# A hybrid encoder layer: the recurrence's inputs scaled in the stage before it, head sums token-major, two inverses in one run

## The chip, the cores and the metric

The kernel runs on one core of one Trainium2 chip. The metric is the device time of one launch in microseconds (us), lower is better. TensorE (PE), VectorE (DVE), ScalarE (ACT) and GpSimd (POOL) each work through their own queue in order. All transfers are issued by SyncE (SP), also in order.

## The reference

One layer of a bidirectional encoder is applied to two groups with shared weights: 1024 prompt tokens and 256 sample tokens, 1280 in all, model width 1024, fp32. What the change touches is the RWKV-7 branch of the token mixer: 8 heads of size 64, a forward and a backward scan with their own decay `w` and rate `a`.

```python
kk = heads(k32 * k_k)
kk = kk / jnp.maximum(jnp.linalg.norm(kk, axis=-1, keepdims=True), 1e-12)
for d, (z, z_shift, rev) in enumerate(...):
    ...
    w = jnp.exp(-jnp.exp(-jax.nn.softplus(-logit) - 0.5))
    a = jax.nn.sigmoid(iclr_a0[d] + za @ iclr_a2[d])
    kd = k32 * (1.0 + (a - 1.0) * k_a)
    outs.append(_wkv_scan(heads(r32), heads(w), kk, kk * heads(a), heads(kd), heads(v32), rev))
# one step of the scan, per head, S is 64 x 64
sa = S @ kk_t
S = S * w_t - sa b_t^T + v_t k_t^T
y_t = S @ r_t
...
bonus = jnp.sum(heads(r32) * heads(k32) * r_k, axis=-1, keepdims=True) * heads(v32)
```

Around it stand the input projection (1024 to 5888 columns), a gated convolution branch, two output projections, a gated ConvFFN and a gated embedding.

## The kernel before, in words

The scan is done in chunks of 64 tokens. Inside a chunk the decays are folded into the inputs: with P the running product of decays, the kernel needs q = r P, c = kk P(previous), k = kd / P and b = -kk a / P. A Gram product of (b, k) with (c, q) gives triangular 64 x 64 matrices. One of them must be inverted. POOL inverts its 32 x 32 diagonal blocks by elimination, 31 multiply-add pairs in a chain; two small PE products fill in the off-diagonal block.

**Stage one** projects and prepares. PE works through a list of blocks (`Fill`): one block is 128 output columns for all 1280 tokens, 72 matmuls into tile `mm`. Between its matmuls the code places other work. `go(us)` runs so much planned fill; `run_side()` empties a list of small closures (`side`) that otherwise go one at a time each `fill.pace` us of fill. For each of the four head pairs `hp` there is a k block and an r block. Then come `lora` products in psum tile `sm` for both directions d and two kinds (0: decay logit, 1: rate a), the sum of squares of kk over each head (`kk_norm`) and the bonus sum (`bonus`). Both sums are PE products of a [128 channels, 1280 tokens] operand, split into high and low halves (`halve`: tiles `gl`, `t`), with a block of ones (`bo`, `ind`). The closures write L (log decay, cumulated by a DVE scan), kd, nb, kk and r to DRAM (`to_in`, tensors d_in and d_kr). The big work tiles of this stage come from a ring `o5` of four, the others from a ring `t5` of three.

**The recurrence** has 20 steps n (10 groups of 128 tokens forward, 10 backward), two chunks in each. A step's own chain alternates small PE products with short copies on ACT and DVE:

- `b_x2`: AT with Dm, copied by ACT; `b_m21`: the result with MT, copied by ACT into MT.
- For each chunk: `c_p1` (tile p, copied to R), `c_sa` (R with MT, copied to SV), `c_z` (SV with ZL; DVE adds it to the state Sc and scales it into the next SV). After the second chunk SP stores the step's output (d_y from Y).
- For later steps: `a_prep` loads X (d_in, d_kr), takes two exponentials on ACT and makes K = (b, k) and LS = (c, q) by seven DVE products. `a_gram(n, h)` makes Gram half h: eight PE products, six masked DVE copies into AT, LS and ZL. `a_t` transposes K. SP sends AT to DRAM (dA) and back in another layout (`load_u`, tiles U and W). POOL runs `b_inv` (tiles tm and W). SP sends W out (dW, `b_out`) and back into MT (`b_back`), and DVE transposes it (`b_d`, tile Dm).

In step n the code places the Gram and the inverse for n+2, the way back of the inverse for n+1, and `a_prep` for n+3. `gap(us)` spreads the fill that is left evenly over the steps (gates and convolution blocks, 72 matmuls each). From step 11 on each step also has a group norm for one finished token group, on DVE and ACT (`gn`, tiles cvp, cvy, gr...), handed out by the second argument of `gap`. Nearly every engine instruction is issued through a wrapper that keeps program order; its one line is L199 before and L205 after, so groups are told apart by their tiles.

Of the kernel before, what the change touches and what calls it, by code (L numbers as in the profile page):

```python
# [12 lines left out]
D = 1024  # L13
# [112 lines left out]
def build(tc, I, O, dbg=None, upto=99):  # L126
# [10 lines left out]
    def to_in(d, nm, hp, t, w=128):  # L137
        dst, o = (d_in[d], 0) if nm in ("L", "kd", "nb") else (d_kr, 386)
        SP.dma_start(dst[hp * 128:(hp + 1) * 128, :, IN[nm][0] - o:IN[nm][1] - o], t.rearrange("p (g t) -> p g t", t=w))
# [27 lines left out]
    d_in = [dram([DC, NT, 386], f"d_in{d}") for d in range(2)]  # L167
    d_kr = dram([DC, NT, 256], "d_kr")
    IN = dict(L=(0, 130), kd=(130, 258), nb=(258, 386), kk=(386, 514), r=(514, 642))
# [38 lines left out]
    wq = pool("wq", 1, side="right")  # L208
    p1 = pool("p1", 1, side="right")
# [84 lines left out]
    class VBlock:  # L294
# [110 lines left out]
    zs, ks, kks, kns, S1 = {}, {}, {}, {}, {}  # L405
# [58 lines left out]
    def halve(nm, t):  # L464
        def hi():
            S1[nm] = sb(p1b, [128, T], F32R, "gl"), sb(p1, [128, T], F32R, "t5", 3)
            A.copy(S1[nm][0], S1[t])
        return [hi, lambda: V.tensor_tensor(S1[nm][1], S1[t], S1[nm][0].bitcast(F32), ALU.subtract)]

    def ones(ps, w, hl):  # L470

        for t0, n in TTS:
            for q in range(2):
                PE.matmul(ps[:, t0:t0 + n], w, hl[q][:, t0:t0 + n], start=q == 0, stop=q == 1)

    def k_block(hp):
# [6 lines left out]
        def done():  # L483
            kk = kks[hp] = sb(p1b, [128, T], F32, "kk", 1)

            def square():
                S1["kk2"] = sb(p1, [128, T], F32, "t5", 3)
                A.activation(S1["kk2"], kk, AF.Square)
            side([lambda: V.tensor_scalar(kk, ks[hp], pc("k_k", hp), None, ALU.mult), square,
                  lambda: to_in(0, "kk", hp, kk)])  # L490
        return Block(OFF["k"] + hp * 128, ev, begin, done)

    def kk_norm(hp):

        ps = sb(psm, [128, 3 * 512], F32, "sm")
        ones(ps, S1["bo"], S1["sq"])
        n2 = kns[hp] = sb(p1, [128, T], F32, "t5", 3)
        V.tensor_scalar(n2, ps[:, 0:T], 1e-24, None, ALU.max)
        side([lambda t=t: V.reciprocal(n2[:, t:t + 320], n2[:, t:t + 320]) for t in range(0, T, 320)])
        side([lambda: V.tensor_tensor(n2, n2, kks[hp], ALU.mult)])  # L500

    def r_block(hp):
        def begin():
            S1["r"] = sb(p1, [128, T], F32, "o5", 4)

        def ev(ps, t0, n, po):
            A.copy(S1["r"][:, t0:t0 + n], ps)

        def done():
            side([lambda: to_in(0, "r", hp, S1["r"])])  # L510
        return Block(OFF["r"] + hp * 128, ev, begin, done)

    def rk_prep(hp):
        def product():
            S1["rkk"] = sb(p1, [128, T], F32, "t5", 3)
            V.scalar_tensor_tensor(S1["rkk"], S1["r"], pc("r_k", hp), ks[hp], ALU.mult, ALU.mult)
        side([product])

    def bonus(hp):

        if hp == 0:
            S1["bn"] = sb(p1b, [128, T], F32, "bn")
        rows = slice(32 * hp, 32 * hp + 32)
        run_side()
        ps = sb(psm, [128, 3 * 512], F32, "sm")
        ones(ps[0:32], S1["ind"], S1["rk"])
        A.copy(S1["bn"][rows], ps[0:32, 0:T])

    def bonus_t(i, n):

        ps = sb(pt, [128, 4, 128], F32, "tp")
        for j in range(n):
            PE.transpose(ps[:, j, :], S1["bn"][:, (i + j) * 128:(i + j + 1) * 128], ident)
        V.tensor_copy(bon[:, i:i + n, :].rearrange("p i (q h) -> p i h q", q=2),
                      ps[:, 0:n, :].rearrange("p i (h x) -> p i h x", x=32)[:, :, :, 0:2])
# [14 lines left out]
    def lora(d, hp, which):  # L550
# [9 lines left out]
        if which == 0:  # L560
            L = sb(p1, [128, NCH, 65], F32, "o5", 4)
# [61 lines left out]
    items[-1].ahead = items[-1].every = 2  # L623
# [3 lines left out]
    for j in range(8):  # L627
# [335 lines left out]
    blocks = sb(wq, [128, 128], F32, "gth", 2)  # L963
    SP.dma_start(cs1, I["consts"][:, C_SCAN:C_BO])
    SP.dma_start(blocks, I["consts"][:, C_BO:C_WI])
    for nm, t in (("bo", blocks), ("ind", ind)):
        S1[nm] = sb(p1b, [128, t.shape[1]], F32R, nm)
        A.copy(S1[nm], t)

    def mix(n, jobs, lead=0.0, used=0.0):  # L970

        go(lead)
        run_side()
        for j in jobs:
            j()
            go((12.6 - lead - used) / len(jobs))
        fill.until(n + 1)

    def rates(hp):

        js = [lambda d=d, w=w: lora(d, hp, w) for d in range(2) for w in range(2)]
        js.insert(2, lambda: rk_prep(hp))
        js.insert(4, lambda: side(halve("rk", "rkk")))
        return js
# [5 lines left out]
    js = [lambda i=i: g_out(i) for i in range(NT)]  # L990
    for d in range(2):
        js.insert(3 + 4 * d, lambda d=d: lora_split(d))
    mix(2, js, 3.0)
    for hp in range(4):
        if hp > 0:
            mix(2 + 2 * hp, rates(hp - 1), 0.9)
        go(1.7)
        if hp > 0:
            bonus(hp - 1)
        side(halve("sq", "kk2"))  # L1000
        mix(3 + 2 * hp, [lambda: kk_norm(hp)], 6.0, 1.7)
# [17 lines left out]
    LS = [sb(wk, [128, 3, 8, 64], F32, f"LS{i}") for i in range(3)]  # L1019
# [1014 lines left out]
```

## Time and profile before

| what | value |
|---|---|
| median of three runs | 2251.77 us (2249.8 to 2258.03) |
| the profiled execution, its own time | 2248.55 us |
| its span, first to last instruction | 2246.8 us |
| mean granted TensorE clock | 0.982 |
| PE busy | 2143.3 us, 95% |
| DVE, ACT, POOL busy | 1455.8, 872.4, 613.0 us |
| first and last `b_x2` product of the recurrence | 354.9 and 920.0 us |

A time is read from the start of the span. In a table of stretches each engine's busy time stands beside its count of instructions, then the granted clock, the share of time the DMA engines were busy, and GB/s. The rows come with the prediction.

### The profile page before, as it was taken

Reading aid. Unit: us, or ns where it says so; the run is one execution under the profiler, and the core shown is the slowest. Engines: PE = TensorE matmul, PEld = TensorE weight load, DVE = VectorE, ACT = ScalarE, POOL = GpSimd, SP = SyncE. Lnnn points to the kernel's source line nnn. Section 1 sums busy time; section 2 is a strip of 40 time slices with the busy share of each in tenths; the row PEclk is TensorE's granted clock in tenths of the full one; section 3 lists DMA queues with packets and bytes.
Section 4 is the critical chain, followed back from the end, with each engine's and each line's share of the span. In section 5 each row is a group of like instructions: output and inputs, shape, how many; then the busy total and the mean of one; then the engine's idle time right before and its main releaser. Section 6 shows DMA issues by size and latency. Waiting matters only on the chain.

```text
span 2246.8 us, 40106 instructions
## 1 busy us (share of the span) xinstructions
PE 2143.3 (95%) x15895; PEld 1855.1 (83%) x15895; DVE 1455.8 (65%) x2325; ACT 872.4 (39%) x1531; POOL 613.0 (27%) x1370
## 2 busy tenths in 40 slices
PE   6999999999999889999997999999999999999998
PEld 5877887878777777888886999999999888887886
DVE  5488845655556775565576687777677755556565
ACT  4533222333344444431444444444444521113444
POOL 3024337888787777100000000000000011115000
PEclk9999999999999999999998999999999999999999
DMA  4456664445456665553445532122212442233121
GB/s 152 125 125 157 160 182 130 115 121 150 138 158 172 198 181 138 183 178 137 141 132 168 146 98 74 62 72 71 73 62 88 139 146 85 85 111 130 43 72 62
DMA packets 333975, 278.58 MB, mean 124 GB/s; under 512 B 93693, under 2 KB 297307, under 8 KB 333787
## 3 DMA queue, kind: packets, MB, share of 16 engines
q1 hardware_dynamic: 333787, 276.01, 41.0%
q8 instruction: 125, 2.05, 0.4%
q14 instruction: 63, 0.52, 0.1%
HBM read 192.50 MB, written 83.44 MB: 123 GB/s over the span
## 4 chain that ended last, share of the span: by engine, by line
PE 54%; DVE 8%; POOL 5%; DMA 4%; issue 3%; ACT 2%; SPq 2%; ACTq 0%; POOLq 0%; DVEq 0%
PE mm L199 22%; PE X L199 12%; PE Y L199 9%; PE g L199 6%; POOL W L199 3%; POOL tm L199 3%; SPq L199 2%; PE p L199 2%; DMA dA<-AT 1%; DVE h L199 1%; DVE wl L199 1%; DVE cvp L199 1%; PE m L199 1%; DVE aj L199 1%; PE tp L199 1%
## 5 line engine op out<-in xcount | busy, mean ns | idle before, releaser
L199 PE MATMUL mm<-U,wh 128*128 128x512 f32 (+1 forms) x1872 | 530.3, 371 | 2.8 <-ACT U L199 2.3
L199 PEld LDWEIGHTS mm<-U,wh 128*128 128x128 f32 x1872 | 326.4, 192 | 64.0 <-issue 3.7
L199 PE MATMUL mm<-U,wl 128*128 128x512 f32 (+1 forms) x936 | 338.4, 362 | 1.0 <-POOL wl L199 1.0
L199 POOL TENSOR_TENSOR MG<-raw,MG 128x1024 fp32r<-128x1024 f32 x5 | 12.1, 2417 | 974.5 <-ACT MG L199 974.5
L199 POOL TENSOR_TENSOR tm<-W,U 128x60 f32<-128x60 f32 (+24 forms) x620 | 225.6, 364 | 122.2 <-DMA W<-in_consts 63.6
L199 POOL TENSOR_TENSOR W<-W,tm 128x60 f32<-128x60 f32 (+24 forms) x620 | 234.6, 378 | 48.6
L199 DVE TENSOR_TENSOR f<-f,mm 128x512 f32<-128x512 f32 x200 | 136.3, 686 | 104.3 <-PE mm L199 103.1
L199 PEld LDWEIGHTS mm<-U,wl 128*128 128x128 f32 x936 | 179.0, 191 | 29.9 <-POOL wl L199 1.5
L199 PE MATMUL mm<-MG,act 128*128 128x512 f32 x600 | 159.9, 393 | 2.0 <-DVE f L199 1.9
L199 DVE SCALAR_TENSOR_TENSOR h<-MGb,fcol,h 128x255 f32<-128x255 f32 (+1 forms) x176 | 152.5, 880 | 14.3 <-ACT h L199 12.5
L199 PE MATMUL X<-B,wh 128*128 128x384 f32 (+1 forms) x936 | 158.4, 315 | 2.6 <-DVE MGb L199 2.6
L199 ACT CAST wh<-raw 128x512 fp32r<-128x512 f32 (+1 forms) x141 | 113.8, 808 | 118.1 <-PE Y L199 41.6
L199 PEld LDWEIGHTS X<-B,wh 128*128 128x128 f32 x936 | 144.2, 189 | 3.2 <-DVE MGb L199 3.2
L199 PE MATMUL X<-B,wl 128*128 128x384 f32 (+1 forms) x804 | 137.1, 315 | 2.9 <-DVE MGb L199 2.9
L199 PEld LDWEIGHTS mm<-MG,act 128*128 128x128 f32 x600 | 113.8, 190 | 26.4 <-DVE f L199 2.6
L199 PEld LDWEIGHTS X<-B,wl 128*128 128x128 f32 x804 | 123.7, 190 | 3.2 <-DVE MGb L199 3.1
L199 PE MATMUL mm<-wh,MG 128*128 128x512 f32 x400 | 126.2, 394 | 0.0
L199 PE MATMUL g<-WG,MG 128*128 128x512 f32 x480 | 112.8, 391 | 0.0
L199 PEld LDWEIGHTS g<-WG,MG 128*128 128x128 f32 x480 | 89.4, 188 | 18.3
L199 DVE TENSOR_TENSOR wl<-raw,wh 128x1024 fp32r<-128x1024 f32 (+1 forms) x68 | 79.7, 1172 | 23.6 <-ACT wh L199 23.3
L199 PEld LDWEIGHTS mm<-wh,MG 128*128 128x128 f32 x400 | 74.8, 187 | 18.4
L199 PE MATMUL Y<-B,wh 128*128 128x384 f32 x420 | 85.1, 335 | 0.0
(494 smaller groups left out, 4274.6 us busy)
## 6 DMA issues: line engine op xcount, KB each, us to landing
raw<-in_w_up SPq DMA_DIRECT2D x53, 512.0 KB
raw<-in_w_in SPq DMA_DIRECT2D x39, 512.0 KB
X<-d_in SPq DMA_DIRECT2D x20, 772.0 KB
d_act<-h SPq DMA_DIRECT2D x22, 640.0 KB
MGb<-d_act SPq DMA_DIRECT2D x20, 640.0 KB
raw<-in_w_down SPq DMA_DIRECT2D x22, 512.0 KB
d_in<-o SPq DMA_DIRECT2D x16, 640.0 KB
X<-d_kr SPq DMA_DIRECT2D x20, 512.0 KB
```

Of the source, the lines that this page charges most:

```text
L199: return lambda *a, **k: tc.keep_in_program_order(f(*a, **k))
```

## The change

Five things change together.

1. **Scaled inputs.** The two exponentials and the products with P and 1/P move from the recurrence (`a_prep`, removed) into stage one (`scaled_inputs`). Stage one stores k and b (d_bk, already in the layout of tile K, in runs of 64 floats) and c and q (d_cq). The recurrence loads K and LS by DMA alone (`load_k`, `load_l`). The end-of-chunk decays stay on chip in `pend`. The multiplications by k and by the normalized kk go from POOL to DVE, three affine steps from DVE to ACT.
2. **Head sums token-major.** `by_head` takes 128 channels x 128 tokens as the stationary operand and two columns of ones as the moving one, ten matmuls for 1280 tokens, in place of `ones` on split halves. The reciprocal then runs on 20 elements of each partition instead of 1280; `kk_norm` spreads it back over the channels by ACT copies and ten PE transposes. `bonus_t` and `halve` are gone.
3. **Two inverses in one run.** U, W and tm hold two steps. `b_inv(m)` does steps 2m and 2m+1 with the same 62 POOL instructions, each twice as large.
4. **Grams three to four steps ahead.** Odd steps make the Grams for n+3 (at the old place) and n+4 (late in the step), even steps none. POOL starts a run at the start of an even step; its result goes out in the odd step.
5. **Two gate blocks** of fill are moved from the recurrence to the time before it.

```diff
+    def by_head(x):
+        ps = sb(pt, [128, 512], F32, "tp")
+        for i in range(NT):
+            PE.matmul(ps[:, 2 * i:2 * i + 2], x[:, i * 128:(i + 1) * 128], ind[:, 0:2], start=True, stop=True)
...
+    def kk_sum(hp):
+        run_side()
+        r = S1["rn"] = sb(p1, [128, NT, 2], F32, "rn")
+        V.tensor_scalar(r, by_head(S1["kk2"]), 1e-24, None, ALU.max)
+        V.reciprocal(r, r)
     def kk_norm(hp):
         ps = sb(psm, [128, 3 * 512], F32, "sm")
-        ones(ps, S1["bo"], S1["sq"])
...
-        side([lambda t=t: V.reciprocal(n2[:, t:t + 320], n2[:, t:t + 320]) for t in range(0, T, 320)])
+        for i in range(0, NT, 4):
+            n = min(4, NT - i)
+            rb = sb(wq, [128, 4, 128], F32, "gth", 2)[:, 0:n]
+            A.copy(rb.rearrange(...), S1["rn"][:, i:i + n].unsqueeze(3).broadcast_to((128, n, 2, 64)))
+            for j in range(n):
+                PE.transpose(ps[:, (i + j) * 128:(i + j + 1) * 128], rb[:, j], ident)
+        V.scalar_tensor_tensor(kns[hp], ps[:, 0:T], -0.5, kks[hp], ALU.mult, ALU.mult)
...
+        def k_out():
+            V.tensor_tensor(S["kd"], S["kd"], S["Pi"], ALU.mult)
+            to_in(d, "k", hp, S["kd"])
...
+        return [affine, lambda: V.scalar_tensor_tensor(a, a, 1.0, kn, ALU.add, ALU.mult),
+                lambda: V.tensor_tensor(S["kd"], S["kd"], k, ALU.mult), inverse, decay, k_out, b_out, q_out, c_out]
...
-            mix(2 + 2 * hp, rates(hp - 1), 0.9)
...
+    rates = lambda d, hp: [(0.9, lambda: lora(d, hp, 0)), (1.5, lambda: lora(d, hp, 1))]
+            rk_prep(hp - 1)
+            mix(2 + 2 * hp, rates(0, hp - 1) + [(8.5, lambda: bonus(hp - 1))])
+        mix(3 + 2 * hp, (rates(1, hp - 1) if hp > 0 else [(2.4, run_side)])
+            + [(3.0, lambda: kk_sum(hp)), (5.0, lambda: kk_norm(hp))])
...
+            G.tensor_tensor(tm[:, :, cs, js], W[:, :, cs, i:i + 1].broadcast_to(shape), Ut[:, :, i:i + 1, js].broadcast_to(shape), ALU.mult)
+            G.tensor_tensor(W[:, :, cs, js], W[:, :, cs, js], tm[:, :, cs, js], ALU.add)
...
+        if not odd:
+            if n + 2 < N:
+                load_u(n // 2 + 1)
+                b_inv(n // 2 + 1)
+            b_back(n + 1)
...
+        if odd and n + 3 < N:
+            a_gram(n + 3, 0)
...
         c_z(n, 1)
+        load_l(n + 4)
+        if nx:
             load_v(n + 2)
-        gap(0.7, 1)
-        side(a_prep(n + 3))
-        gap(4.2)
+            if odd:
+                b_out(n // 2 + 1)
+                b_back(n + 1)
+        gap(4.9, 1)
+        if odd and n + 4 < N:
+            for h in range(2):
+                a_gram(n + 4, h)
+        gap(3.0)
         if nx:
             b_d(n + 1)
-        gap(6.7, 1)
+        gap(3.7, 1)
```

DVE in stage one, the second direction of one head pair, before (SCALAR_TENSOR_TENSOR with `cs` is the scan; `t_1273` is the norm of the next pair, `o_1134` L, `o_1171` a, `o_1172` kd):

```order
L199 TENSOR_SCALAR o_1134<-o_1134 128x20x64
L199 SCALAR_TENSOR_TENSOR o_1134<-cs_588,o_1134 128x1300
L199 TENSOR_TENSOR t_1153<-t_1125,gl 128x1280
L199 TENSOR_SCALAR o_1172<-o_1171,half 128x1280
L199 TENSOR_SCALAR o_1171<-o_1171 128x1280
L199 TENSOR_SCALAR kk<-k,pcol 128x1280
L199 TENSOR_TENSOR t_1234<-t_1216,gl 128x1280
L199 TENSOR_TENSOR wl<-raw,wh 128x1024
L199 TENSOR_SCALAR t_1273<-sm 128x1280
L199 RECIPROCAL t_1273<-t_1273 128x320 x4
L199 TENSOR_TENSOR t_1273<-t_1273,kk 128x1280
```

The same place after (`o_1220` is L and then q, `o_1241` a and then b, `o_1246` kd and then k, `cvy` 1/P and then c, `o_1269` P, `rn` the 20 norms):

```order
L205 SCALAR_TENSOR_TENSOR o_1220<-cs_590,o_1220 128x1300
L205 SCALAR_TENSOR_TENSOR o_1241<-o_1241,t_1038 128x1280
L205 TENSOR_TENSOR wl<-raw,wh 128x1024
L205 TENSOR_TENSOR o_1246<-o_1246,k 128x1280
L205 TENSOR_TENSOR o_1246<-o_1246,cvy 128x1280
L205 TENSOR_TENSOR o_1241<-o_1241,cvy 128x1280
L205 TENSOR_TENSOR o_1220<-cvp,o_1269 128x1280
L205 TENSOR_TENSOR cvy<-kk,o_1269 128x1280
L205 TENSOR_SCALAR rn<-tp 128x20
L205 RECIPROCAL rn<-rn 128x20
L205 SCALAR_TENSOR_TENSOR t_1339<-sm,kk 128x1280
```

The long reciprocal is gone, and the two small instructions on `rn` now stand behind the five products of the second direction.

ACT at the same place after (`kk` and `t_1208` are kk and its square for the next pair, `sm,half` the two tanh that empty `sm`):

```order
L205 ACTIVATE kk<-k,pcol 128x1280
L205 ACTIVATE t_1208<-kk 128x1280
L205 ACTIVATE o_1220<-sm,half 128x20x64
L205 ACTIVATE o_1220<-o_1220 128x20x64
L205 CAST wh<-raw 128x1024
L205 ACTIVATE o_1241<-sm,half 128x1280
L205 ACTIVATE o_1246<-o_1241,half 128x1280
```

Before, kk came from DVE; now kk and its square stand on ACT ahead of the tanh that frees `sm` for the second product.

SP in the second half of an odd step, after (LS is loaded in three pieces; dW and MT are the inverse's way out and back, dA the late Gram's way out):

```order
L205 DMA K<-d_bk_58 128x4x256
L205 DMA d_thr<-gth 128x256
L205 DMA d_y_64<-Y 64x2x256 x2
L205 DMA LS_2206<-d_cq_60 64x4x128 x2
L205 DMA LS_2206<-d_cq_60 128x4x128
L205 DMA SV<-d_v 64x2x256 x2
L205 DMA dW<-W 512x1x32 x4
L205 DMA MT_2207<-dW 32x8x32 x4
L205 DMA dA<-AT 32x8x32 x4
```

Before, dW and MT stood ahead of d_y in every step and the X loads behind SV; now the load that the late Gram needs stands behind the step's own store.

More of the change, by code (lines that the diff above doesn't have):

```diff
@@ L165, in build @@
     dram = lambda shape, tag: dr.tile(shape, F32, name=tag, tag=tag)
[L167 to L169 removed]
+    d_bk = [dram([DC, NT, 256], f"d_bk{d}") for d in range(2)]
+    d_cq = [dram([DC, NT, 256], f"d_cq{d}") for d in range(2)]
     d_v, d_g = dram([2, T, 256], "d_v"), dram([2, T, 256], "d_g")
@@ L208, in build @@
     wq = pool("wq", 1, side="right")
+    pend = sb(wq, [128, 2, 4, NCH], F32, "pend")
     p1 = pool("p1", 1, side="right")
@@ L462, in g_out @@
         SP.dma_start(d_g[:, tk, :].rearrange("q t m -> t q m"), gt.rearrange("t (q m) -> t q m", q=2))
[L464 to L474, printed above, removed]
+    def by_head(x):
+        ps = sb(pt, [128, 512], F32, "tp")
+        for i in range(NT):
+            PE.matmul(ps[:, 2 * i:2 * i + 2], x[:, i * 128:(i + 1) * 128], ind[:, 0:2], start=True, stop=True)
+        return ps[:, 0:2 * NT].rearrange("p (i q) -> p i q", q=2)
     def k_block(hp):
@@ L515, in product @@
             S1["rkk"] = sb(p1, [128, T], F32, "t5", 3)
-            V.scalar_tensor_tensor(S1["rkk"], S1["r"], pc("r_k", hp), ks[hp], ALU.mult, ALU.mult)
+            V.scalar_tensor_tensor(S1["rkk"], rs_[hp], pc("r_k", hp), ks[hp], ALU.mult, ALU.mult)
         side([product])
     def bonus(hp):
-        if hp == 0:
-            S1["bn"] = sb(p1b, [128, T], F32, "bn")
-        rows = slice(32 * hp, 32 * hp + 32)
         run_side()
[L525 to L535, printed above, removed]
+        V.tensor_copy(bon.rearrange("p i (q h) -> p i q h", q=2)[:, :, :, hp], by_head(S1["rkk"]))
     def lora_load(d):
@@ L622, in build @@
         items += [k_block(hp), r_block(hp)]
-    items[-1].ahead = items[-1].every = 2
+    items += [gate(0, 0), gate(1, 0)]
+    items[-1].ahead, items[-1].every = 20, 1
     items += [VBlock(0), VBlock(1)]
@@ L626, in build @@
         items += conv(i)
-    for j in range(8):
+    for j in range(1, 8):
         items += [gate(0, j), gate(1, j)]
@@ L962, in build, with mix @@
     cs1 = sb(p1b, [128, 1300], F32, "cs1")
-    blocks = sb(wq, [128, 128], F32, "gth", 2)
     SP.dma_start(cs1, I["consts"][:, C_SCAN:C_BO])
[L965 to L974, printed above, removed]
+    def mix(n, jobs):
+        for us, j in jobs:
+            go(us)
             j()
-            go((12.6 - lead - used) / len(jobs))
         fill.until(n + 1)
[L979 to L984, printed above, removed]
     fill.until(2)
@@ L1303, in group_norm @@
         SP.dma_start(d_ob[tk, :], y2)
-    load_x(0)
-    go(17.0)
-    side(a_prep(0))
-    run_side()
-    go(5.0)
-    for h in range(2):
-        a_gram(0, h)
-        go(1.2)
-    load_u(0)
-    b_inv(0)
-    a_t(0)
-    go(1.2)
-    side(a_prep(1))
-    go(11.0)
-    run_side()
-    for h in range(2):
-        a_gram(1, h)
-        go(1.2)
-    load_u(1)
-    a_t(1)
-    go(1.2)
-    go(8.0)
+    load_k(0)
+    for n in range(4):
+        load_l(n)
+    go(6.0)
+    for n in range(4):
+        for h in range(2):
+            a_gram(n, h)
+            go(1.2)
+        if n == 1:
+            load_u(0)
+            b_inv(0)
+        if n < 3:
+            a_t(n)
+            load_k(n + 1)
+            go(6.0)
+    go(5.0)
     b_out(0)
     b_back(0)
-    b_inv(1)
-    side(a_prep(2))
-    go(10.0)
-    b_d(0)
-    go(2.0)
-    fill.until(12)
+    fill.until(14)
     load_v(0)
@@ L1337, in build @@
     go(4.0)
+    b_d(0)
     gn = iter(())
```

228 lines of the change are left out of this document (109 added, 119 removed).

## The prediction

> **What bounds the kernel now.** I read the table of slices first (PE is busy 95% of the span), then stretches, since only two stages are touched: stage one (about 108 to 300 us) and the recurrence (355 to 950 us). Columns: length, busy time and count of PE, PEld, DVE, ACT and POOL, granted clock, DMA share, GB/s.
>
> ```profile
> core 0: us, PE busy (x) PEld busy (x) DVE busy (x) ACT busy (x) POOL busy (x), PEclk, DMA share, GB/s
> 150.00:193.00 43.00, 38.71 (x180) 30.04 (x179) 36.31 (x20) 14.46 (x16) 15.15 (x6) 0.96 0.59 145
> 193.00:236.00 43.00, 39.31 (x181) 30.41 (x181) 40.67 (x22) 15.97 (x18) 15.17 (x6) 0.96 0.64 148
> 236.00:300.00 64.00, 61.01 (x440) 56.37 (x441) 37.82 (x27) 16.15 (x21) 14.20 (x5) 0.95 0.68 177
> 355.00:671.00 316.00, 304.27 (x3914) 245.46 (x3912) 181.16 (x346) 111.98 (x251) 253.81 (x690) 0.98 0.51 135
> 671.00:950.00 279.00, 258.48 (x3139) 208.67 (x3139) 177.63 (x358) 127.75 (x255) 174.44 (x475) 0.95 0.61 174
> 413.00:440.00 27.00, 26.31 (x354) 21.37 (x353) 19.32 (x32) 9.30 (x21) 22.77 (x55) 1.00 0.39 109
> 585.00:590.00 5.00, 3.74 (x59) 3.52 (x60) 3.34 (x6) 1.10 (x3) 4.29 (x10) 0.81 0.52 122
> 590.00:595.00 5.00, 5.00 (x101) 4.08 (x100) 2.37 (x6) 2.26 (x6) 3.98 (x14) 0.85 0.91 295
> 1000.00:1050.00 50.00, 50.00 (x260) 42.75 (x259) 30.40 (x52) 10.18 (x19) 0.00 (x0) 1.00 0.35 120
> ```
>
> PE bounds nearly all of it, so only PE's idle time and lost clock can be won, or PE work. In the recurrence PE idles 11.7 + 20.5 us, and the clock costs .02 x 316 + .05 x 279 = 20.3 us: 52.5 us in all. In stage one it idles 4.3 + 3.7 + 3.0 us, and the clock costs .04 x 86 + .05 x 64 = 6.6 us: 17.6 us. DVE, 40.67 of 43 us busy in the second stretch, is what is late there. An undisturbed step (413 to 440) takes 27.0 us; 595 us over 20 steps is 29.7. The next view groups PE's waits by what ended them (total, times, longest), the first five of the recurrence, the last three of stage one.
>
> ```profile
> DVE Dm L199 <- DMA MT<-dW: 74.5, 36, 6.8
> PE g L199 <- ACT X L199: 8.1, 3, 3.6
> PE p L199 <- DVE SV L199: 7.1, 6, 2.4
> PE g L199 <- DVE LS L199: 5.3, 2, 3.9
> PE g L199 <- DVE Dm L199: 4.5, 5, 1.7
> ...
> PE sm L199 <- ACT gl L199: 6.6, 3, 2.6
> PE sm L199 <- DVE t L199: 5.1, 6, 1.5
> PE sm L199 <- ACT o L199: 1.2, 2, 1.0
> ```
>
> In the recurrence the waits hang on DVE: SV, LS and Dm come late, and Dm itself waits 74.5 us for the inverse's way back, with DVE's later work queued behind it. In stage one the sums wait 6.6 + 5.1 + 1.2 = 12.9 us for the split halves and for `sm`, 4.3 for each of three head pairs.
>
> **Stage one, priced.** Groups by form (count, total us and mean ns, idle time before), one DVE row and one PE row of the time line:
>
> ```profile
> L199 DVE RECIPROCAL t<-t 128x320 f32<-128x320 f32 x12 | 24.6, 2110 | 0.1
> L199 DVE TENSOR_TENSOR_SCAN o<-cs,o 128x1300 f32<-128x1300 f32 x8 | 22.9, 2866 | 0.8
> L199 DVE TENSOR_SCALAR kk<-k,pcol 128x1280 f32<-128x1280 f32 x3 | 10.7, 3583 | 0.0
> L199 DVE TENSOR_TENSOR t<-t,kk 128x1280 f32<-128x1280 f32 x4 | 6.0, 1491 | 0.1
> L199 ACT ACTIVATE o<-sm,half 128x1280 f32<-128x1280 f32 x15 | 20.0, 1332 | 38.5 <-DMA d_in<-o 17.4 <-PE sm L199 11.0 <-issue 5.0
> L199 ACT ACTIVATE t<-kk 128x1280 f32<-128x1280 f32 x3 | 3.8, 1276 | 21.8 <-DVE kk L199 21.8
> L199 ACT COPY gth<-mm 128x512 f32<-128x512 f32 x7 | 4.0, 585 | 13.2 <-PE mm L199 12.6 <-DMA d_v<-gth 0.6
> 212.06 1.22 DVE L199 TENSOR_TENSOR wl<-raw,wh 128x1024 fp32r<-128x1024 f32 x1
> 292.00 1.60 PE L199 MATMUL mm<-ZL,U 128*128 128x256 f32 x12
> ```
>
> (a) PE work. A large matmul takes 50.00 / 260 = .192 us. `ones` was 4 x 2 x 3 matmuls for each sum: 48 x .192 = 9.2 us go, with ten transposes of `bonus_t`. `by_head` adds 80 products and `kk_norm` 40 transposes. No row shows two moving columns; the nearest small ones are the twelve matmuls in 1.60 us, .13 each. 120 x .13 - 9.2 - 1.3 = **+5**. The other bounds are .192 each (the large matmul, +12.5), and 0, if they only fill what is now idle.
>
> (b) Two gate blocks, 2 x 72 x .192 = 27.6 us, leave the recurrence and enter ahead of it: **0** in the sum.
>
> (c) The norm of pairs 1 to 3 becomes a chain through three engines. From the first lora product of direction 1: ACT does kk and its square (1.28 each) ahead of the tanh (1.33), so `sm` comes free at 3.9, while PE wants it at 2.5: a wait of 1.4. Then L + 1 on ACT (1.3) to 5.2; DVE's scan (2.87), a product (1.49), `wl` (1.22) and five more products (7.45) to 18.2; the two small ones (under .4) and the first ACT copy (.58) to 19.2. PE reaches the first transpose after its planned fill, 14.9 us on: a wait of 4.3, and part of one more copy. About 6 us against 4.3 now, three times: **+5**. DVE loses 8.2 us of reciprocal and 3.6 of kk for each pair and gains products of 1.5; if these run ahead of ACT the wait vanishes (-13). (d) The clock there then stays as it is: **0**.
>
> (e) The tail. The last L needs a tile of the ring of four whose q is still being stored; ACT now spends 17.4 us waiting for such stores (its row, d_in<-o). I take 5 us there and 3 us until the first Gram has its K, against the 3.0 idle us and 2 us of clock of 236 to 300 now: **+3**; 0 if the stores are quick, +8 if one takes the mean of that wait, 17.4 / 3 = 5.8, twice.
>
> **The recurrence, priced.** Tile rows (shortest, median, longest ns), then the time line of two step ends: issues on SP, and what waited for them.
>
> ```profile
> L199 DVE TENSOR_TENSOR K<-X,Pi x80: 640/689/832, 297.7 to 858.4; 64x512 f32<-64x512 f32 x80
> L199 DVE TENSOR_TENSOR LS<-X,P x60: 672/693/831, 298.9 to 860.9; 64x512 f32<-64x512 f32 x40, 128x512 f32<-128x512 f32 x20
> ...
> 757.79 1.80 SPq L199 DMA_DIRECT2D MT<-dW  x4
> 760.14 1.27 SPq L199 DMA_DIRECT2D d_y<-Y  x2
> 760.91 0.44 DVE L199 STREAM_TRANSPOSE Dm<-MT 32x256 f32<-32x256 f32 x1 [0.54 <-DMA MT<-dW]
> 766.51 0.50 SPq L199 DMA_DIRECT2D X<-d_kr  x1
> 776.20 0.37 ACT L199 COPY Y<-y 128x256 f32<-128x256 f32 x1 [2.23 <-PE y L199]
> 782.02 0.42 SPq L199 DMA_DIRECT2D W<-in_consts  x1
> 786.13 0.65 POOL L199 TENSOR_TENSOR tm<-W,U 128x31 f32<-128x31 f32 x1 [2.54 <-DMA W<-in_consts]
> ```
>
> (f) DVE loses 80 x .689 + 60 x .693 = 96.7 us in the recurrence, nearly all of it beside PE's work: it counts only through the 52.5 us. What stays or is new:
> - The late Gram of eight odd steps needs LS. SP issues LS behind the step's own store: Y copy .37, d_y 1.27, three loads of .5, so issued 3.1 us after `c_z`. Landing takes 1.3 us by MT (759.59 to 760.91) or 3.7 by W (782.44 to 786.13). PE arrives after 4.1 us of fill: a wait of .3 to 2.7. I take 1.3, a little under the middle: 10 us.
> - `b_d` behind the Gram's copies on DVE, .5 x 8 = 4. Even steps lose the Gram between `b_m21` and `c_sa`; .7 us of fill is left where ACT's copy and hand-over want 1: 5 over ten steps. SV, 7.1 now: 3.
> - Clock. At 585 to 595 a loss of 1.26 us of PE work cost .19 x 5 + .15 x 5 = 1.7 us. If half of the eight Gram waits do that, 7.
>
> That leaves 29 of 52.5: **-23.5**; bounds 0 (it all comes back) and -45 (only `b_d` and SV stay).
>
> The Trainium skill, "TensorE: Matmul & The Clock Gate", section "What's actually happening", says that the clock halves only after at least one idle window of about 3.4 us. The trace disagrees: the clock was .81 and .85 around 1.26 us of idle. By the page the Gram waits would cost no clock, and the sum would come out 7 us lower, near 2231.
>
> (g) POOL. A run for two steps must end within a pair. Rows of the run from 724 to 751 us:
>
> ```profile
> 717.68 0.21 POOL L199 TENSOR_TENSOR tm<-W,U 128x8 f32<-128x8 f32 x1
> ...
> 724.09 0.24 POOL L199 TENSOR_TENSOR tm<-W,U 128x31 f32<-128x31 f32 x1 [5.80 <-DMA d_thc<-gth]
> 733.30 0.33 POOL L199 TENSOR_TENSOR tm<-W,U 128x76 f32<-128x76 f32 x1
> 749.98 0.66 POOL L199 TENSOR_TENSOR W<-W,tm 128x8 f32<-128x8 f32 x1
> ```
>
> 62 instructions take 26.5 us now. Between 8 and 76 elements they grow by .12 us, .0018 per element; about 50 more in each of 62 adds 5.6: 32 us. The ends are 26.5 (size costs nothing) and 53 (time goes with size); the rows of different size lie near the first. The run starts some 6.5 us into an even step, U and W landing as W does above, and its result is sent out 18.7 us into the odd one: 37 to 38 us. It fits: **0**.
>
> **Sum.** 5 + 0 + 5 + 0 + 3 - 23.5 + 0 = -10.5, rounded to -10. Against the profiled execution's 2248.55 us: 2238.5. That execution lies 3.2 below the median of 2251.77, and I leave this in the range. A measurement of this kernel tells about .5%, 11 us, from no change.
>
> **Rivals.**
> - A, the sum: 2226 to 2250 by its own terms. Chance .45.
> - B, a larger gain. LS lands in 1.3 us, so the Gram waits (10) and their clock (7) go, and the norm's chain is no longer than before (5): 2238.5 - 22 = 2216, own range 2200 to 2226. For it: MT's row, and the DVE time taken out of stage one. Against: LS is far larger than MT. Chance .24.
> - C, nothing net. LS lands as W does, 2.7 x 8 = 22 in place of 10, with clock for each: 2238.5 + 12 + 3 = 2253, own range 2248 to 2258. For it: W's row. Chance .16.
> - D1, slower by one wait, at the norm's transposes. Each us beyond 6 costs 3; the gain is gone at 6 + 10 / 3 = 9.3 us a pair. DVE would have to run its products slowly, as kk's 3583 ns shows (a product is 1491): three of them give 6 + 3 x 2.1 = 12.3, so 2238.5 + 19 = 2257 to 2265. Against: kk's slow row falls beside POOL's products, which go. Chance .08.
> - D2, slower by the POOL run. Beyond 38 us each us costs one on each of nine pairs; it decides at 38 + 10 / 9 = 39. At 53 it is + 135, 2373. Against: the rows of 8 and 76 elements. Chance .07.
>
> **The numbers.** Time 2238.5, A's sum. Faster by over .5% is below 2240.5: B's .24, .27 of A's .45: .51. Slower is above 2263: D2 and some of D1 and C: .13. The rest, .36, is within. Range 2200 to 2262: it reaches into B (below 2200 some .05) and C, and leaves out D2 and half of D1 (.11).
>
> **What the profile after would show.** (a) PE busy in stage one a few us up beyond the gate blocks. (c) Three waits of PE's `sm` for ACT's `gth` of about 4 us, and none for `gl`; waits that are absent make B. (e) ACT waiting for q's store near the end of stage one. (f) Eight waits of PE's `g` for LS's load, about 1.3 us (nothing: B; 2.7: C), DVE's wait for MT far below 74.5 us, and clock in the recurrence above .96. (g) POOL runs of about 32 us, no wait of `b_d` or x2 beyond 1 us. The forecast is wrong if DVE's row in stage one stays near 40 of 43 us, if PE's idle time in the recurrence does not fall from 32 us to about 22, or if a step pair takes over 58 us.

## The result and the profile after

The changed kernel takes 2285.7 us (median of four runs, 2282.4 to 2291.03) against 2251.76 us (median of four runs, one more than in the table above): 1.0148 of the kernel before, 95% interval 1.012 to 1.0176. The forecast was 2238.5, range 2200 to 2262. The profiled execution after took 2291.03 us, the slowest of its four, so its 42 us over the profiled 2248.55 us of before are a little more than the medians' 34.

The stretches of both kernels are cut at the same events: from stage one to 291 us (where the changed PE runs dry), from there to the first `b_x2`, and the recurrence in two parts up to the last `b_x2`. Before:

```profile
108.00:291.00 183.00, 169.09 (x919) 138.59 (x918) 146.56 (x82) 58.99 (x64) 59.65 (x23) 0.96 0.60 148
291.00:354.90 63.90, 61.21 (x447) 53.89 (x446) 33.26 (x60) 13.60 (x22) 32.27 (x93) 1.00 0.57 165
354.90:671.00 316.10, 304.37 (x3915) 245.56 (x3914) 181.26 (x346) 111.98 (x251) 253.91 (x690) 0.98 0.51 135
671.00:919.60 248.60, 228.07 (x2814) 184.12 (x2815) 164.05 (x334) 112.53 (x224) 174.44 (x475) 0.95 0.61 169
```

After:

```profile
108.00:291.00 183.00, 174.16 (x899) 142.10 (x898) 113.76 (x83) 95.67 (x107) 0.93 (x7) 0.96 0.54 131
291.00:397.40 106.40, 81.10 (x690) 76.75 (x691) 29.48 (x62) 14.21 (x23) 25.91 (x66) 0.87 0.60 143
397.40:714.80 317.40, 302.45 (x3879) 244.47 (x3880) 133.32 (x259) 99.05 (x227) 148.07 (x354) 0.97 0.52 128
714.80:959.60 244.80, 221.38 (x2766) 177.64 (x2766) 135.37 (x281) 106.39 (x211) 101.21 (x217) 0.95 0.58 155
```

The first `b_x2` comes 42.5 us later, and this is made up as follows (the terms are rounded):

- 8.6 us are moved work. PE is busy 523.8 us in the recurrence after, 532.4 before, mostly since one more step's Gram now stands ahead of it (7.3 us of products into tile `g`).
- 10.1 us are the head sums and the way back of the norm, which cost PE more than before (rows under (a) below).
- PE's idle time falls by 5.1 us up to 291 us and rises by 22.6 us from there on (25.3, before 2.7).
- The last 6.4 us go with the clock, .87 between the stages against 1.00: the fill products (tile `mm`) ahead of the first `b_x2` take 268.6 us where they took 262.2, for 1437 records where there were 1433.

So the fill ahead of the recurrence did not grow, although two gate blocks were put there. The kernel before had run as much other fill in that time, and the recurrence has 1648 records of `mm` products where it had 1654.

The recurrence itself takes 562.2 us, 2.5 less than the 564.7 of before, although it has 8.6 us less PE work: it idles 15.0 + 23.4 us, before 11.7 + 20.5. DVE is 77 us less busy there, and in this run the recurrence is hardly shorter for it.

Three places carry the idle time. First, PE's wait before the first Gram, and the chain that ended in it (start, length, what; in order of time):

```profile
310.54 2.08 PE L205 MATMUL g<-LS,K 64*128 64x128 f32 x16 [19.33 <-DMA LS<-d_cq]
...
274.99 7.48 DMA d_cq<-cvy
282.56 1.28 ACT cvy L205
...
291.48 7.15 DMA d_cq<-o
...
304.77 5.74 DMA LS<-d_cq
310.54 2.08 PE g L205 x16
```

The last pair's second direction must wait for `cvy`, which still holds c of the first direction while it is stored (7.48 us); then come its exponentials and products, its own store (7.15), then K and twelve LS loads on SP, and the landing (5.74). SP's rows of that time:

```profile
291.48 1.93 SPq L205 DMA_DIRECT2D d_cq<-o  x1
...
298.82 0.95 SPq L205 DMA_DIRECT2D gnw<-in_gn_w  x2
...
300.91 0.56 SPq L205 DMA_DIRECT2D K<-d_bk  x1
301.52 9.73 SPq L205 DMA_DIRECT2D LS<-d_cq  x12
```

Second, the late Gram of the odd steps. SP's rows of the first one, PE's Gram, and the group of all Gram products of the recurrence (its last column: idle time before them, and what ended most of it):

```profile
439.09 1.25 SPq L205 DMA_DIRECT2D d_y<-Y  x2
440.40 1.91 SPq L205 DMA_DIRECT2D LS<-d_cq  x3
446.25 3.15 PE L205 MATMUL g<-LS,K 64*128 64x128 f32 x26 [2.88 <-DMA dW<-W]
L205 PE MATMUL g<-LS,K 64*128 64x128 f32 x512 | 41.6, 316 | 18.3 <-issue 8.6 <-DMA LS<-d_cq 4.7 <-DMA dW<-W 2.9
```

LS is issued by 442.31 and used from 446.25 on, 3.9 us later. The releaser named is the last semaphore event near it; the load is what the Gram reads. The eight late Grams wait 1.67 to 2.88 us each, 18.3 us in all.

Third, Dm of the last pairs. SP at the start of step 14 (749.2 us), POOL's run for steps 16 and 17, and PE at step 18:

```profile
749.82 0.33 SPq L205 DMA_DIRECT2D d_ob<-cvp  x1
754.32 0.89 SPq L205 DMA_DIRECT2D cvp<-d_y  x2
756.27 2.77 SPq L205 DMA_DIRECT2D U<-dA  x4
759.09 1.96 SPq L205 DMA_DIRECT2D W<-in_consts  x2
768.16 0.74 POOL L205 TENSOR_TENSOR tm<-W,U 128x62 f32<-128x62 f32 x1 [38.56 <-DMA MT<-dW]
932.35 0.31 PE L205 MATMUL g<-Dm,AT 32*32 32x32 f32 x2 [9.80 <-DVE Dm L205]
```

U's load stands behind the group norm's load of `cvp`, which waits 4 us for the previous group norm's store to land. So POOL starts 19 us into the step, and at the last pair PE waits 9.8 us.

### The profile page after: what moved, and what is told of

Its sections match the earlier page's. It is cut to its first block, busy times and chain, and to the rows that moved or that the text cites. A ratio compares the mean times of both kernels' runs of the same rounds, so it can differ in the third digit from the quotient of the medians.

```text
span 2289.2 us, 39504 instructions
## 1 busy us (share of the span) xinstructions
PE 2164.9 (95%) x16037; PEld 1876.2 (82%) x16037; DVE 1338.6 (58%) x2186; ACT 889.3 (39%) x1533; POOL 368.9 (16%) x734
## 4 chain that ended last, share of the span: by engine, by line
PE 68%; DMA 6%; DVE 5%; POOL 4%; issue 3%; ACT 2%; SPq 2%; ACTq 0%; DVEq 0%; POOLq 0%
PE mm L205 31%; PE X L205 13%; PE Y L205 10%; PE g L205 8%; PE p L205 3%; PE m L205 3%; POOL W L205 2%; POOL tm L205 2%; SPq L205 2%; DMA MT<-dW 1%; PE y L205 1%; DMA LS<-d_cq 1%; DVE wl L205 1%; PE tp L205 1%; DMA d_ob<-cvp 1%
## 5 line engine op out<-in xcount | busy, mean ns | idle before, releaser
L205 PE MATMUL mm<-U,wh 128*128 128x512 f32 (+1 forms) x1872 | 536.3, 374 | 3.0 <-ACT U L205 2.3
L205 POOL TENSOR_TENSOR tm<-W,U 128x120 f32<-128x120 f32 (+24 forms) x310 | 135.5, 437 | 354.1 <-DMA MT<-dW 182.8
L205 ACT CAST wh<-raw 128x512 fp32r<-128x512 f32 (+1 forms) x141 | 113.8, 808 | 112.5 <-PE Y L205 41.6
L205 POOL TENSOR_TENSOR W<-W,tm 128x120 f32<-128x120 f32 (+24 forms) x310 | 139.2, 449 | 24.3
L205 DVE TENSOR_TENSOR AT<-g,cst 64x256 f32<-64x256 f32 x80 | 33.7, 421 | 133.0 <-PE g L205 131.5
L205 PEld LDWEIGHTS g<-WG,MG 128*128 128x128 f32 x480 | 89.4, 188 | 18.3
L205 PE MATMUL g<-LS,K 64*128 64x128 f32 x640 | 54.2, 323 | 43.6 <-DMA LS<-d_cq 24.0
```

What stands on the lines that cost most here:

```text
L205: return lambda *a, **k: tc.keep_in_program_order(f(*a, **k))
```

## Experiments

Ratios are to runs of the kernel before on the same chip; a change against the changed kernel's 1.0148 is the quotient of the two.

### LS ahead of the second `c_z`

```diff
+        load_l(n + 4)
         gap(1.5, 1)
         c_z(n, 1)
-        load_l(n + 4)
```

> The LS load is issued before the second c_z instead of behind it and the step's own store, about 4 us earlier on SP. Theory 2 (the eight late Grams of the odd steps wait 19 us in all, 1.8 to 3.05 each, because LS is issued behind d_y): the eight waits fall below 0.5 us each, half of their lost clock comes back too (about 5 us): 2285.7 - 24 = about 2262 us (2256 to 2270). Rival (what holds the load is bandwidth, not its place): the waits fall by half at most, 2275 to 2280 us. Second rival (the Gram is then on time but DVE's tail and b_d wait instead): 2280 to 2287 us.

Measured: 2266.63 us, 1.0056 (1.0038 to 1.0074), so .991 of the changed kernel, 21 us less. SP, the Gram and the group of all Grams in this run:

```profile
436.23 1.89 SPq L205 DMA_DIRECT2D LS<-d_cq  x3
440.43 1.25 SPq L205 DMA_DIRECT2D d_y<-Y  x2
444.64 2.06 PE L205 MATMUL g<-LS,K 64*128 64x128 f32 x32
L205 PE MATMUL g<-LS,K 64*128 64x128 f32 x512 | 35.0, 281 | 0.8 <-DMA LS<-d_cq 0.8
```

The waits fall from 18.3 to .8 us, and the Grams take 35.0 in place of 41.6 us, since they no longer run at half clock. Theory 2 holds; the place on SP's queue was the cause, not bandwidth.

### U ahead of the group norm's loads

```diff
             b_back(n + 1)
+        if n >= 11:
+            gl_g = steps[n - 1][1]
+            gl_t = gn_load(gl_g)
...
-        if n >= 10:
-            gl_g = steps[n][1]
-            gl_t = gn_load(gl_g)
```

> From step 11 on, the group norm's loads go to SP behind the loads of U and W instead of ahead of them. Theory 3 (POOL's runs start 19 us into the even steps instead of 9, since U waits on SP behind a group norm load that waits for the previous group norm's store to land; so the last two runs end late and x2 waits 10 + 3 us): POOL starts within 11 us of the start of steps 14, 16 and 18, the waits of x2 for Dm at 867 and 922 us go, with 7 us of clock: 2285.7 - 18 = about 2268 us (2262 to 2275). Rival (the group norm's first product then waits on DVE for its own loads and holds SV behind it): 2283 us or more.

Measured: 2275.38 us, 1.0084 (1.0061 to 1.0108), 14 us less than the changed kernel. SP and POOL at step 14 (742.7 us here):

```profile
743.42 2.79 SPq L205 DMA_DIRECT2D U<-dA  x4
746.25 0.90 SPq L205 DMA_DIRECT2D W<-in_consts  x2
750.70 1.91 SPq L205 DMA_DIRECT2D cvp<-d_y  x2
753.01 0.29 POOL L205 TENSOR_TENSOR tm<-W,U 128x62 f32<-128x62 f32 x1 [30.51 <-DMA cvp<-d_y]
```

POOL starts 10 us into the step and no longer 19, and PE's waits for Dm in the last pairs fall from 2.8 and 9.8 us to 1.5 and 1.6. Theory 3 holds, though 14 us came back and not 18: U and W still need 6 us from issue to POOL.

### Both of them

> LS before c_z and U before the group norm's loads, the place between the stages as in the changed kernel. If the two losses inside the recurrence are separate (- 21 and - 14): 2285.7 - 35 = about 2251 us (2245 to 2257), the time of the kernel before, so that what the recurrence gains (first b_x2 to last about 530 us in place of 562) pays for what is lost ahead of it. If they share a cause: 2258 to 2266 us.

Measured: 2252.47 us, .9987 (.9973 to 1.0002): the time of the kernel before. What lies ahead of the recurrence from 291 us on, and its two parts:

```profile
291.00:399.20 108.20, 83.42 (x706) 78.86 (x704) 29.89 (x63) 15.75 (x24) 25.91 (x66) 0.87 0.59 143
399.20:708.00 308.80, 305.16 (x4068) 245.79 (x4068) 138.40 (x272) 102.91 (x237) 157.21 (x373) 1.00 0.55 136
708.00:924.50 216.50, 209.85 (x2576) 168.54 (x2576) 132.27 (x270) 102.44 (x201) 93.84 (x198) 0.96 0.64 170
```

The two losses add. The recurrence now takes 525.3 us, 39 less than in the kernel before, with 10.3 us of idle time and a clock of 1.00 and .96. This about pays for the 44 us by which it starts later.

### More fill before the first Gram

Two tries to cover the chain with work, the second with gate blocks in place of V blocks.

```diff
-    go(6.0)
+    go(25.0)
```

> 19 us more fill (go 6 to go 25) before the first Gram; nothing else changes, and the fill up to block 14 ahead of the recurrence stays the same. Theory 1 (the changed kernel loses 19.3 us at the first Gram, because its K and LS loads stand behind the last stores of the scaled inputs and PE has nothing planned for that time): the wait falls below 3 us, the first b_x2 comes at about 383 us in place of 397, and the time is 2285.7 - 13 = about 2273 us (2264 to 2277). Rival (the wait only moves on: POOL's first run then sets when the recurrence starts, or the recurrence lacks the fill): the recurrence starts within 5 us of 397, 2280 to 2287 us.

Measured: 2289.66 us, 1.0153 (1.0128 to 1.0179): nothing. PE's wait moved, and POOL's first run came later:

```profile
302.47 0.58 PE L205 MATMUL mm<-cvy,U 128*128 128x256 f32 x1 [8.47 <-ACT cvy L205]
359.67 0.29 POOL L205 TENSOR_TENSOR tm<-W,U 128x62 f32<-128x62 f32 x1 [86.39 <-DMA d_v<-gth]
396.24 0.31 PE L205 MATMUL g<-Dm,AT 32*32 32x32 f32 x2 [3.22 <-DVE Dm L205]
```

The fill is V blocks, and their weights are split into `cvy`, which the last store still reads. So theory 1 fell in its simple form: what PE could do meanwhile hangs on the same store. POOL's first run starts at 359.7 in place of 342.9 and then the first `b_x2` waits for it.

```diff
-    items += [gate(0, 0), gate(1, 0)]
+    items += [gate(0, 0), gate(1, 0), gate(0, 1), gate(1, 1)]
```

> The changed kernel with two more gate blocks (27.6 us of fill) moved ahead of the V blocks, and 25 in place of 6 us of fill before the first Gram (as in the run with more fill, where PE then waited 8.6 us for a V block's weight tile that shares `cvy` with the last store of c, and POOL's first run started 17 us later). Theory 1b (the loss of 20 us between the stages is the serial chain last lora, products, store, landing, reuse of its memory, load; V blocks hang on the same store, gate blocks don't): no wait over 3 us between 285 and 345 us, the recurrence takes 27 us less from its first to its last step, since that fill is gone from it, and the time is 2285.7 - 22 = about 2264 us (2256 to 2272). Rival (the steps of the recurrence are bound by their own chain and don't get shorter without fill): 2280 us or more.

Measured: 2300.41 us, 1.0213 (1.0196 to 1.023), worse. One wait is left between 285 and 345 us, and it is for a store of gate output:

```profile
319.94 0.79 PE L205 MATMUL mm<-U,wh 128*128 128x256 f32 x2 [16.83 <-ACT gth L205]
```

ACT waited 21.7 us for d_thr, whose store stood on SP behind the group norm's constants, K and twelve LS loads. With that queue cut short (LS of the first step alone ahead of the Gram, the rest behind):

> The run with two more gate blocks ahead of the V blocks (2300.4 us), with the same shorter queue. There PE waited 17 us at 302.7 for a gate tile whose store stood on SP behind gn's constants, K and twelve LS loads (ACT waited 21.7 us for d_thr). If that queue is why fill could not cover the chain: this wait falls below 6 us, and the time to about 2300 - 14 = 2286 us (2280 to 2291); it does not reach 2264, since the recurrence shortened by less than the fill it lost. If fill is held by the same stores and not by the queue: 2296 to 2303 us.

Measured: 2294.6 us, 1.0188 (1.0162 to 1.0214). The wait falls to 5.1 us as expected, the time by only 6 us in place of 14, and the two intervals overlap: PE then waits 7.3 us for LS of a later Gram, where the run before this one waited 5.7 us for K. Nor does fill that leaves the recurrence shorten it by as much: with 20.0 us less PE work than in the changed kernel it takes 552.7 us, 9.5 less, and PE idles 48.8 us in it in place of 38.4.

### What makes the chain

Four runs cut at the chain itself: a shorter load queue; the last pair stored early; both; the last stores on another queue.

```diff
-    for n in range(4):
-        load_l(n)
+    load_l(0)
...
             load_k(n + 1)
+            load_l(n + 1)
```

> The changed kernel, with SP's queue between the stages made shorter: ahead of the first Gram only its own LS (3 of 12 loads), each further LS beside the K of its step, the four loads of the group norm's constants behind the Grams. Theory 1c (the 19.5 us before the first Gram are one serial chain of last lora, products, stores, landing, load; the queue is only its last piece): the first Gram starts 4 to 6 us earlier and the K waits of the next Grams stay: 2285.7 - 6 = about 2280 us (2275 to 2284). Rival (the twelve loads hold up K, LS and the gate stores, so the queue is most of it): the wait falls below 8 us, 2265 to 2273 us.

```diff
+        if (d, hp) == (1, 3):
+            for nm, t in (("k", k), ("b", kn), ("q", r), ("c", kk)):
+                to_in(d, nm, hp, t)
+            return [affine, decay, lambda: A.copy(pend[:, d, hp, :], S["P"][:, :, end])]
```

> The changed kernel with one part of the computation left out: for the last head pair of the second direction k, b, q and c are stored as they are, without the products with P and 1/P, as soon as the last lora product is issued. The same bytes are stored; 12 of some 400 us of ACT and DVE work go; the last stores no longer hang on scan, exponentials and products. Theory 1c (the loss between the stages is that chain, some 35 us from the last lora product to the first Gram, with 17 us of fill beside it): the first Gram waits under 6 us in place of 19.5, no 20 us of half clock, and the time is 2285.7 - 13 to 20 = about 2269 us (2264 to 2274). Rival (the stores' and loads' own time and SP's queue make the wait): the wait stays above 12 us, 2277 us or more.

> Both cuts together: the last pair of the second direction stored unscaled at once (that part of the computation is left out), and only K and the first LS loaded ahead of the first Gram. Each alone left 14.2 to 14.6 us of the 19.5. Theory 1d (two chains of nearly equal length end at the same place, products with stores and landing on one side, SP's queue of stores and loads on the other): together they leave 4 to 8 us, and the time is 2285.7 - 11 = about 2275 us (2270 to 2279). Rival (one floor under both, the landing of stores and loads): the wait stays above 11 us, 2280 us or more.

PE's wait before the first Gram in the three runs, in this order:

```profile
308.96 2.08 PE L205 MATMUL g<-LS,K 64*128 64x128 f32 x16 [14.05 <-DMA raw<-in_w_in]
307.65 2.08 PE L205 MATMUL g<-LS,K 64*128 64x128 f32 x16 [14.48 <-DMA LS<-d_cq]
302.68 2.08 PE L205 MATMUL g<-LS,K 64*128 64x128 f32 x16 [9.73 <-DMA d_thr<-gth]
```

The times: 2282.86 (1.0134, 1.0111 to 1.0157), 2283.58 (1.0129, 1.0111 to 1.0147) and 2282.46 us (1.0133, 1.0114 to 1.0151). The queue and the chain of products each take 5 us off the wait, and together 10: the two follow one another. The wait falls less than the theories asked for (below 6 us with the early stores, 4 to 8 with both): half of it stays, and it was not taken apart further. The time falls by only 2 to 3 us, inside the intervals. The gain does not reach the recurrence: its first `b_x2` comes at 398.7, 396.0 and 392.9 us, and at 395.0 to 399.2 in the runs that leave this place alone, since PE waits for LS or K before the next Grams; and the last pair then waits 12.7 to 12.8 us for Dm in place of 9.8. In the second run SP's issues alone hold 44.4% of the chain from 260 to 320 us: SP has something to issue nearly all the time, and the stores in short runs take 1 to 2 us of it each.

```diff
+        Q = A if hp == 3 else SP
-            SP.dma_start(d_cq[d][hp ...
+            Q.dma_start(d_cq[d][hp ...
```

> The changed kernel, complete, with the twelve stores of head pair 3 (both directions) issued by ACT in place of SP, so that SP is free for gate stores, weights, K and LS. Theory 1d: SP no longer issues for 28 us in a row; the chain of products, store and landing is left: the wait before the first Gram falls from 19.5 to 12 to 16 us, 2285.7 - 5 = about 2281 us (2275 to 2284). Rival 1 (the queue is the whole of it): below 9 us, under 2275. Rival 2 (ACT now stands in its issues while PE needs its evictions): 2286 to 2296 us.

Measured: 2292.76 us, 1.0175 (1.0158 to 1.0192). Rival 2: ACT stands in its own issues, and PE waits for its `sm`, before the wait at the Gram:

```profile
272.07 5.34 ACTq L206 DMA_DIRECT2D d_bk<-o  x4
283.10 1.43 PE L206 MATMUL sm<-za,lw1h 128*128 128x512 f32 x3 [6.94 <-ACT o L206]
317.00 2.08 PE L206 MATMUL g<-LS,K 64*128 64x128 f32 x16 [13.71 <-DMA LS<-d_cq]
```

### Everything together

> The three edits together. If the three losses are separate they add up: 2285.7 - 13 - 24 - 18 = about 2231 us (2222 to 2243), below the kernel before (2251.8). If they share a cause, or another wait takes over once they go (POOL's run of two steps, DVE): 2245 to 2262 us.

Measured: 2259.69 us, 1.0018 (1.0004 to 1.0031). This is 7 us more than the two edits alone: 25 us of fill delay POOL's first run to 357.8 us, and the first step takes 31.8 us in place of 25.3.

The next run has, beside these three edits, the two more gate blocks ahead of the V blocks (in the changed kernel alone 2300.41 us):

> The last one together with the earlier LS load and with U ahead of the group norm's loads. If the three losses are separate: 2259.7 (the three edits before) - 20 = about 2240 us (2230 to 2249), under the kernel before (2254.9 beside those runs). If the steps can't use the time: 2255 to 2262 us.

Measured: 2275.78 us, 1.01 (1.0084 to 1.0116); the recurrence has 498.0 us of PE work, 17 less than with the two edits alone (515.0), and takes 524.6 us, .7 less. That is above both ranges: beside the three edits the two gate blocks cost about 18 us (1.01 and 1.0018).

> The three edits (LS before c_z, U before the group norm's loads, more fill before the first Gram, here 16 us in place of 25) with the shorter queue, to see whether a version gets below the kernel before (2251.8 to 2254.9). With the three edits alone 2259.7 us; there POOL's first run started at 357.8 and the first b_x2 waited 3.4 us for it with 13.7 us of half clock behind. If K and LS land sooner, POOL starts near 347 and that goes: 2259.7 - 11 = about 2249 us (2242 to 2255). If the V blocks' weight tile and the K loads still hold PE: 2256 to 2261 us.

Measured: 2246.37 us, .9975 (.9962 to .9988), the fastest of all and, by its interval, .1 to .4% under the kernel before. POOL's first run starts at 344.8 again, and the first `b_x2` at 392.0:

```profile
291.00:392.00 101.00, 82.63 (x700) 77.86 (x698) 29.23 (x62) 15.53 (x24) 24.20 (x66) 0.92 0.58 147
302.43 0.58 PE L205 MATMUL mm<-cvy,U 128*128 128x256 f32 x1 [7.13 <-ACT cvy L205]
```

> The fastest version so far (LS before c_z, U before the group norm's loads, 16 us of fill and only the first loads ahead of the first Gram; 2246.4 us, .9975 of the kernel before) with the same twelve stores on ACT. If SP's queue still holds up the V blocks' tile and K there (7.3 and 9.1 us of PE waits): 2246.4 - 6 = about 2240 us (2234 to 2245). If not, or if ACT's evictions suffer: 2246 to 2254 us.

Measured: 2251.71 us, .9992 (.9982 to 1.0003). PE's wait for the V block's tile falls from 7.1 to 1.5 us, so SP's queue did hold that tile up. But PE now waits 3.3 us for `sm` behind ACT, and 2.4 and 8.6 us for LS where it waited 8.9, and nothing is won. Whether it is a loss stays open: the interval just overlaps that of the run without the ACT stores.

### The run of two steps at single size

```diff
+            for q in (slice(0, 1), slice(1, 2)):
+                shape = (128, 1, cs.stop - cs.start, js.stop - js.start)
-                G.tensor_tensor(tm[:, :, cs, js], ...
+                G.tensor_tensor(tm[:, q, cs, js], ...
```

> The changed kernel with POOL's run of 62 double-size instructions replaced by 124 of single size, same place and same result. It prices the pairing and tells how much room the run has. If the run is at the edge of its window (theory 3: start 9 to 19 us into the even step, needed 19 us into the odd one, so about 36 us fit): a run takes 53 to 56 us in place of 30 to 35, each of nine pairs grows by 17 to 20 us, 2285.7 + 150 to 180 = 2435 to 2465 us, and x2 of the odd step's successor waits for Dm at every pair. If there is room that the traces don't show: under 2350 us.

Measured: 2368.92 us, 1.0514 (1.0493 to 1.0535), 83 us over the changed kernel, half of what was expected and between the two ranges. PE's wait for the last run:

```profile
1009.31 0.31 PE L205 MATMUL g<-Dm,AT 32*32 32x32 f32 x2 [21.48 <-DVE Dm L205]
```

The ten runs take 43 to 48 us on the time line, not 53 to 56, against 30 to 35 paired. About 14 us more of POOL cost 9 us a pair, so about 5 us of room were left: pairing the inverses is worth its price, and the run is near the edge of its window.

## Why the prediction was wrong

- **(a) PE work, twice the forecast.** Forecast +5, measured +10.1, inside the bounds. The first two rows are `by_head` and the transposes after, the others everything on `sm`, before and after. The lora products on `sm` are the same 96 in both, so the old sums took 38.8 - (32.2 - 7.1) = 13.7 us and bonus' transposes 1.6: 18.3 + 7.1 - 13.7 - 1.6 = 10.1.

```profile
L205 PE MATMUL tp<-cst,t 128*128 128x2 f32 x160 | 18.3, 247 | 0.0
L205 PE MATMUL sm<-cst,gth 128*128 128x128 f32 x40 | 7.1, 319 | 7.1 <-ACT gth L205 7.1
100.00:330.00 230.00, 38.84 (x144) 0.97 0.60 154
100.00:330.00 230.00, 32.17 (x136) 0.93 0.59 140
```

Both prices were too low. The old sums cost 13.7 and not 9.2 us. Each of the 80 products of `by_head` stands in the trace as two records and takes 18.3 / 80 = .23 us, not .13. One sum now takes PE 2.29 us; an undisturbed one before took 1.3 (268.5 to 269.9 us). What the token-major form saves is on DVE, not on PE. PEld is busy 3.28 of 3.50 us around one such sum (264.0 to 267.5), so its price may be that of the weight loads; no run separates this.
- **(b) The gate blocks, 0, right**, though they did not leave the recurrence as I had it: its `mm` products stayed (1648 records, before 1654).
- **(c) The norm's chain, wrong in sign.** The row of the transposes has the waits for `gth`: 7.1 us, 6.2 of them in the three pairs, where about 18 were forecast. PE's idle time up to 291 us fell from 13.9 to 8.8 us. The chain itself was as long as I had it: the first transpose starts 19.0 us after the first lora product of direction 1 in each of the three pairs (19.2 forecast), here from 184.05 us:

```profile
203.09 2.25 PE L205 MATMUL sm<-cst,gth 128*128 128x128 f32 x10 [3.09 <-ACT gth L205]
```

The step that failed is PE's own arrival: it came 16.0 to 17.5 us on and not 14.9, 1 us of it the longer `by_head`. And the 1.4 us for `sm` did not come: the second lora product followed at 3.2 us without a wait. (d), the same clock there, was right.
- **(e) The tail, 3 forecast and about 29 measured.** "I take 5 us there and 3 us until the first Gram has its K", net +3. PE waited 19.3 us before the first Gram, then 4.2 for a K, and lost clock: 22.6 us of idle time and 6.4 of clock more than before. The step that failed is that I priced two waits of a chain and not its length: store, exponentials, products, store, release of memory, K and LS on SP, landing. I also took planned fill for cover without asking whose tiles and whose queue it needs. The runs on this place show that the products and SP's queue make up 5 us of the wait each and that the fill hangs on a tile the store still reads. What makes the other half of the wait stays open, and so does what each part costs in the total time (2 to 3 us, inside the intervals).
- **(f) The recurrence.** Forecast -23.5; it came out at -2.5, and about +6 without the moved work. The term that failed first is the late Gram's wait, "I take 1.3, a little under the middle". It was 18.3 / 8 = 2.3, near the upper end of 2.7 by W's landing, as in rival C. Its clock, 7 us, was sized right: with the waits gone the Grams take 6.6 us less. With LS moved ahead, 21 us came back. DVE lost 345.3 - 268.7 = 76.6 us between the first and the last `b_x2`; the 96.7 of the forecast count all 20 steps, and three of these were prepared earlier in the kernel before.
- **(g) POOL.** The run's length was right: 32 forecast, 30 to 35 measured. Its window was not: I let it start 6.5 us into an even step, and it started 7 to 9 us in, and 19 from step 14 on, since I had not followed U past the group norm's loads on SP. I had D2's mechanism, a run that ends too late, but on its length. This cost 14 us.
- **The sum.** Forecast -13 against the median, measured +34: 47 us apart. Between the two profiled spans (+42.4) the terms are 10.1 for (a), -5.1 for (c), 29.0 for (e), 6.1 for (f) with (g), and 2.4 behind the recurrence, where the forecast had 5, 5, 3 and -23.5. So (e) and (f) failed by about as much; the misses of (a) and (c), +5 and -10, went opposite ways, which was luck. The LS wait and U's place are 35 us by experiment. With both mended the recurrence gained 39 us (31 beyond the moved work), more than the 23.5 forecast. This fits the mechanism of (f), hidden by two queue places; no run separates DVE's share in it from the paired inverses and the earlier Grams.
- **The clock.** By the rule of the Trainium skill ("TensorE: Matmul & The Clock Gate", "What's actually happening"), weighed in the prediction, no wait of under 3.4 us would cost clock. The late Grams speak against it: around five of the eight waits the clock dropped (to .67 once and .79 four times, over 8 us). Three stretches:

```profile
443.00:451.00 8.00, 5.12 (x37) 4.36 (x36) 3.97 (x8) 0.00 (x0) 0.00 (x0) 0.67 0.53 119
624.00:632.00 8.00, 6.33 (x52) 5.12 (x52) 4.55 (x12) 0.10 (x1) 0.00 (x0) 1.00 0.55 119
554.00:562.00 8.00, 5.19 (x47) 4.18 (x46) 2.77 (x7) 1.27 (x2) 0.00 (x0) 1.00 0.58 137
```

The first is a wait of 2.88 us; the second, with 1.67 us of idle time, kept its clock. The third is from the run with the early store and the short queue: a wait of 2.81 us, and the clock stayed at 1.00, while another of 2.84 us in that run gave .79. So the length of a wait alone does not decide it, and no threshold can be read from these rows.

## What to carry to other kernels

When work moves ahead of a stage, write down the whole chain from its last input to the first use in the next stage, with every store, release of a tile, issue and landing, and ask of the fill beside it which tiles and which queue it needs itself. When a load decides a term, follow it through its queue: what stands ahead of it, and what that waits for. Two places on SP's queue were worth 35 us here; while they stood, 77 us less of DVE work hardly shortened the recurrence. And price a new form of instruction from a row of the same form, or run it once: a product of two columns cost nearly twice what one of 256 columns had suggested.

## What the hardware showed

Filling the time with more work can make a kernel slower: the two gate blocks put ahead of the V blocks cost .6%, 13 us, beside the run with the same fill and without them (1.0213 and 1.0153 of the kernel before). Their own output leaves through SP's queue, and PE waited 16.8 us for it; with that queue cut short the wait fell to 5.1 us and about 6 us came back, so the queue is at most a part of the price. A product of a 128 x 128 stationary operand with two columns took .23 us. POOL's single-size instructions took 43 to 48 us for 124, less than twice the 26.5 us of one run in the kernel before; there DVE was busier, but no run here separates the two.
